# The v projection of layer 1 as seven products: differences of token rows in place, an earlier load of the second weights, and sums in pairs ahead of their splits

## The chip, the cores and the metric

One core of a Trainium2 chip runs the whole program. The metric is the device time of one execution in microseconds (us). The engines are named as in the profile: PE is TensorE (its matmuls), PEld its weight loads, DVE is VectorE, ACT is ScalarE, POOL is GpSimd, SP is SyncE, which only issues DMAs here. Each engine works through its own queue in order, and semaphores make one wait for another.

## The reference, cut to what matters

The program is a trunk of two layers over 1024 tokens of width 1024. The change touches the beginning of layer 1, where `v` is projected, and the end of layer 0 only in so far as it prepares that.

```
def rms_norm(x, g):
    y = xf * lax.rsqrt(jnp.mean(xf * xf, axis=-1, keepdims=True) + EPS)
    return (y * g.astype(jnp.float32)).astype(x.dtype)
...
            x = x + y @ w_out_a[j]          # end of layer 0
        else:
            h = rms_norm(x, norm_c[j])
            z = h @ w_in_c[j]               # 1024 x 6144
            u, v, g = split_cols(z, (GMLP_WIDTH, GMLP_WIDTH, GMLP_WIDTH))
            v = layer_norm(v, ln_v_g[j], ln_v_b[j])
```

## The kernel before, in words

All large products are kept in float32 accuracy by splitting each operand into a high part in fp32r and the rest (`hi` by an ACT cast, `lo` by a DVE subtraction), and by three matmuls for each product (`mm3`, lines 143 to 146).

**The output projection of layer 0** (`winograd`, lines 737 to 857) uses seven products of quarter matrices where eight would be plain, in 14 turns of 48 matmuls. In its last turns the residual rows `x1` become final. `x1_done` (line 991) stores a finished token tile of 128 rows to `x1dram`, has ACT square and sum it, and leaves the root (POOL) and the multiplication `norm_mul` (DVE, in place, line 187) to `norms_step`, which runs behind later groups of matmuls. Tiles 0 to 3 are finished first and are transposed for layer 1 by `norm_c_transpose` (into `gh` and `gl`). Tiles 4 to 7 are finished in the last turn, 13.

**The v projection** (`v_chunk`, lines 1122 to 1162) runs twice (`vc` 0 and 1), each time for 1024 of the 2048 columns and again with seven products in place of eight. A product has 48 matmuls of 128 x 512: four token tiles (`m`) by four slices of depth by three. I number them P0 to P6. P0 and P1 take the transposed tokens of tiles 0 to 3 (b11, b21); P2 to P6 take t1, t2, b22, t3 and t4, where t1 is the difference of tiles 4 to 7 and tiles 0 to 3 in the first half of the depth, b22 the second half of tiles 4 to 7, t2 = b22 - t1, t3 = t2 - b11 and t4 = b21 - t2. They are made while the products run:

- `token_tile(c)` (line 1085), behind each `m` of P0, takes a DVE difference `diff` of two rows, eight PE transposes into two PSUM banks (`ptd`), an ACT copy of t1 (`t1w`), t2 on DVE, and the splits of t1, b22 and t2.
- `token_less(i, c)` (line 1104) makes t3 (`i` = 2) or t4 (`i` = 3) for one tile with two DVE subtractions and a split.
- `make(i)` (line 1027) makes the weights of product `i` before product `i`-1 starts: for products 2 to 5 a DVE sum of quarters of `w_in_c`, then the split, for each of two halves `j` in turn.
- `fetch` (line 1016) loads the quarters of `w_in_c`: a12, a22, a21, and "sum", which holds the values of a21 at first and is overwritten with the running sums.

The order on ACT, DVE, POOL and SP is the order in which the code issues it (`manual_schedule`), and PE's is the program order. The two dictionaries `steps` (lines 1218 to 1238) say behind which product and token tile each helper is issued.

Of the kernel before, what the change touches and what calls it, by code (L numbers as in the profile page):

```python
# [62 lines left out]
def trunk_kernel(  # L63
# [945 lines left out]
    def v_weights(vc):  # L1009
# [6 lines left out]
        def fetch(*names):  # L1016
            for name in names:
                if name == "sum":
                    whole = big_tile(F32, f"vx{vc}").rearrange("p (j k s) -> p j k s", j=2, k=2)
                    q["sum"] = load_quarter(lambda j: whole[:, j], w_in_c, 0, nh + 1)  # L1020
                else:
                    d, kh = int(name[1]) - 1, int(name[2]) - 1
                    q[name] = load_quarter(
                        lambda j: late["vp"].tile([P, 2, 512], F32, tag="braw", name=f"v{vc}{name}_{j}", bufs=4),
                        w_in_c, kh * 512, nh + d)
# [96 lines left out]
    def v_chunk(vc, ops, steps):  # L1122
# [11 lines left out]
        for i, (bank_set, adds, bop, (d, th), act) in enumerate(products):  # L1134
# [4 lines left out]
            for m in range(4):  # L1139
# [18 lines left out]
                if i in (1, 6):  # L1158
# [1 line left out]
                if i in (5, 6):  # L1160
                    stats(*((0, 1) if i == 5 else (1, 1)), m)
                run(steps.get((i, m), []))
# [308 lines left out]
```

## Time and profile before

| | |
|---|---|
| median of 3 runs | 1345.37 us (1344.26 to 1346.29) |
| the profiled execution: its time | 1346.6 us |
| its span (first to last instruction) | 1344.9 us |
| PE busy | 1307.4 us, 97% of the span |
| PEld, DVE, ACT, POOL busy | 81%, 72%, 51%, 18% |
| mean granted clock of PE | 0.992 of full speed |

The profiled execution took 1.2 us more than the median of the runs, and 1.7 us lie around its span. PE is the engine that nearly fills the span. A stretch of the timeline matters for the time in so far as PE stands idle in it or is granted less than its full clock (1.0 is 2.4 GHz, 0.5 is 1.2 GHz).

### The profile page before, as it was taken

Reading aid. Unit: us, or ns where it says so; the run is one execution under the profiler, and the core shown is the slowest. Engines: PE = TensorE matmul, PEld = TensorE weight load, DVE = VectorE, ACT = ScalarE, POOL = GpSimd, SP = SyncE. Lnnn points to the kernel's source line nnn. Section 1 sums busy time; section 2 is a strip of 40 time slices with the busy share of each in tenths; the row PEclk is TensorE's granted clock in tenths of the full one; section 3 lists DMA queues with packets and bytes.
Section 4 is the critical chain, followed back from the end, with each engine's and each line's share of the span. In section 5 each row is a group of like instructions: output and inputs, shape, how many; then the busy total and the mean of one; then the engine's idle time right before and its main releaser. Section 6 shows DMA issues by size and latency. Waiting matters only on the chain.

```text
span 1344.9 us, 16867 instructions
## 1 busy us (share of the span) xinstructions
PE 1307.4 (97%) x6247; PEld 1091.4 (81%) x6247; DVE 974.2 (72%) x1571; ACT 691.7 (51%) x1245; POOL 236.5 (18%) x240
## 2 busy tenths in 40 slices
PE   7999999999999999999969999999999999999998
PEld 6988888888878888788757788788888888888887
DVE  6568787877678898978757856676666656579874
ACT  6467777786497786344443332444434444433431
POOL 3346565655223222000000000000000000000000
PEclk9999999999999999999979899999999999999999
DMA  6111010211311106313311523413333233596131
GB/s 224 32 48 53 27 54 26 57 39 33 97 33 51 36 17 254 125 61 127 126 63 63 171 80 118 149 67 113 103 110 106 75 110 102 183 372 243 48 110 63
DMA packets 99982, 133.41 MB, mean 99 GB/s; under 512 B 5163, under 2 KB 68796, under 8 KB 97852
## 3 DMA queue, kind: packets, MB, share of 16 engines
q1 hardware_dynamic: 99900, 132.34, 29.5%
q8 instruction: 49, 0.80, 0.3%
q14 instruction: 33, 0.27, 0.1%
HBM read 107.13 MB, written 25.19 MB: 98 GB/s over the span
## 4 chain that ended last, share of the span: by engine, by line
PE 70%; DVE 16%; ACT 8%; issue 3%; DMA 2%; SPq 0%; POOL 0%; DVEq 0%; ACTq 0%
PE m L144 6%; PE m L146 6%; PE m L145 6%; PE u L145 4%; PE u L146 4%; PE u L144 4%; PE g L144 4%; PE g L145 4%; PE g L146 4%; PE v L145 3%; PE v L144 3%; PE v L146 3%; PE s L1352 2%; DVE e L548 2%; PE gb L146 1%
## 5 line engine op out<-in xcount | busy, mean ns | idle before, releaser
L144 PE MATMUL m<-wh_w,wa 128*128 128x512 f32 x432 | 168.6, 390 | 1.4 <-DVE x L851 1.4
L146 PE MATMUL m<-wh_w,wa 128*128 128x512 f32 x432 | 168.1, 389 | 0.0
L145 PE MATMUL m<-wl_w,wa 128*128 128x512 f32 x432 | 168.1, 389 | 0.0
L144 PEld LDWEIGHTS m<-wh_w,wa 128*128 128x128 f32 x432 | 81.1, 188 | 19.0 <-ACT wa L716 1.8
L146 PEld LDWEIGHTS m<-wh_w,wa 128*128 128x128 f32 x432 | 81.1, 188 | 16.8
L145 PEld LDWEIGHTS m<-wl_w,wa 128*128 128x128 f32 x432 | 81.1, 188 | 16.6
L723 ACT CAST wh_w<-b 128x1024 fp32r<-128x1024 f32 x36 | 37.7, 1048 | 74.7 <-DVE b L818 54.2
L548 DVE CUSTOM_DVE_ANT_0 e<-ps,e,sink_bc 128x256 f32<-128x256 f32 (+1 forms) x128 | 61.9, 520 | 3.1 <-POOL e L523 2.6
L564 ACT ACTIVATE e<-e,nm 128x256 f32<-128x256 f32 (+1 forms) x128 | 61.4, 481 | 0.0
L851 DVE TENSOR_TENSOR x<-m,x 128x512 f32<-128x512 f32 x56 | 36.5, 684 | 29.2 <-PE m L146 29.2
L133 DVE TENSOR_TENSOR wl<-raw,wh 128x1024 fp32r<-128x1024 f32 x34 | 45.7, 1350 | 16.1 <-ACT wh L132 15.8
L1324 ACT ACTIVATE sg<-sg 128x512 f32<-128x512 f32 x24 | 15.2, 632 | 70.5 <-DVE sg L1323 70.5
L572 POOL TENSOR_TENSOR e<-e 128x512 f32<-128x512 f32 x28 | 37.2, 1327 | 80.3 <-ACT e L564 80.3
L144 PE MATMUL pq<-hh,wh 128*128 128x512 f32 x128 | 50.4, 394 | 0.0
L144 PE MATMUL ga<-hh,wh 128*128 128x512 f32 x128 | 50.1, 392 | 0.3 <-ACT z L871 0.3
L144 PE MATMUL gb<-hh,wh 128*128 128x512 f32 x128 | 50.1, 391 | 0.0
L724 DVE TENSOR_TENSOR wl_w<-b,wh_w 128x1024 fp32r<-128x1024 f32 x36 | 46.2, 1283 | 5.3 <-ACT wh_w L723 5.1
L146 PE MATMUL pq<-hh,wl 128*128 128x512 f32 x128 | 49.9, 390 | 0.0
L145 PE MATMUL pq<-hl,wh 128*128 128x512 f32 x128 | 49.9, 390 | 0.0
L146 PE MATMUL gb<-hh,wl 128*128 128x512 f32 x128 | 49.9, 390 | 0.0
L145 PE MATMUL gb<-hl,wh 128*128 128x512 f32 x128 | 49.9, 390 | 0.0
L146 PE MATMUL ga<-hh,wl 128*128 128x512 f32 x128 | 49.9, 389 | 0.0
(406 smaller groups left out, 3864.1 us busy)
## 6 DMA issues: line engine op xcount, KB each, us to landing
raw<-in_w_in_a_dram SPq DMA_DIRECT2D x34, 512.0 KB, 4.1
b<-in_w_out_a_dram SPq DMA_DIRECT2D x22, 512.0 KB, 3.5
b<-in_w_out_c_dram SPq DMA_DIRECT2D x22, 512.0 KB, 6.0
vdram<-v SPq DMA_DIRECT2D x32, 256.0 KB, 2.1
rawg<-in_w_in_c_dram SPq DMA_DIRECT2D x16, 512.0 KB, 4.7
rawu<-in_w_in_c_dram SPq DMA_DIRECT2D x16, 512.0 KB, 3.5
vg<-vdram SPq DMA_DIRECT2D x8, 1024.0 KB, 6.0
ydram<-ug SPq DMA_DIRECT2D x32, 256.0 KB, 2.4
```

Source lines behind the costliest of these rows:

```text
L133: nc.vector.tensor_tensor(out=lo, in0=raws[j], in1=hi.bitcast(F32), op=ALU.subtract)
L144: nc.tensor.matmul(acc, lhsT=lh, rhs=rh, start=first, stop=False, skip_group_check=shared)
L145: nc.tensor.matmul(acc, lhsT=lh, rhs=rl, start=False, stop=False, skip_group_check=shared)
L146: nc.tensor.matmul(acc, lhsT=ll, rhs=rh, start=False, stop=last, skip_group_check=shared)
L548: nc.vector.tensor_tensor_reduce(out=e[:, h, k0:256], in0=acc[:, j * 256:j * 256 + kw], in1=e[:, h, k0:256], scale=rs[:, 2 * (b % 4) + j:2 ...
L564: nc.scalar.activation(out=e[:, h], in_=e[:, h], func=AF.Exp, bias=st["nm"][:, h:h + 1], accum_out=st["sums"][:, h:h + 1])
L572: nc.gpsimd.tensor_tensor(out=p, in0=p, in1=e[:, :, P:256], op=ALU.add)
L723: nc.scalar.copy(out=hi, in_=src)
L724: nc.vector.tensor_tensor(out=lo, in0=src, in1=hi.bitcast(F32), op=ALU.subtract)
L851: nc.vector.tensor_tensor(out=dst, in0=accs[m], in1=dst, op=add)
L1324: nc.scalar.activation(out=c, in_=c, func=AF.Silu)
L1352: nc.tensor.matmul(acc[:, i * P:(i + 1) * P], lhsT=vgs[g][:, half * 4 + i, d * P:(d + 1) * P], rhs=ws_t[:, g, :], start=True, stop=True)
```

## The change

It does five things, for both chunks where both have them:

1. The difference of token rows is taken in place, on the first 512 columns of tiles 4 to 7, by the new `norm_c_finish`, directly behind their `norm_mul`. `token_tile` no longer has `diff`; its transposes read `x1` alone.
2. The quarter a12, the weights of P1, is loaded at turn 11 of the output projection, together with a11, into the large tile that "sum" had; "sum" goes to the smaller pool after the rows' stores. a21 is later loaded over a12, one product earlier than before.
3. `make(1)` is issued behind the second token tile instead of ahead of P0.
4. In `token_tile` the four splits stand in another order: b22's cast directly behind the copy of t1, t1's split later.
5. In `make` both halves are summed before both are split, and `token_less` takes several tiles, makes all their sums and then splits them, at fewer places. In P5 and P6 the layer norm's statistics (`stats`) change places, and stand behind the helpers.

```diff
+    def norm_c_finish(t, xt, r):
+
+        norm_mul(xt, xt, r, late["gain_c"])
+        if t >= 4:
+            nc.vector.tensor_tensor(out=xt[:, :512], in0=xt[:, :512], in1=x1_row(t - 4)[:, :512], op=ALU.subtract)
...
-                if name == "sum":
-                    whole = big_tile(F32, f"vx{vc}").rearrange("p (j k s) -> p j k s", j=2, k=2)
-                    q["sum"] = load_quarter(lambda j: whole[:, j], w_in_c, 0, nh + 1)
...
+                d, kh = (1, 0) if name == "sum" else (int(name[1]) - 1, int(name[2]) - 1)
+                if name == "a12":
+                    q["whole"] = big_tile(F32, f"vx{vc}").rearrange("p (j k s) -> p j k s", j=2, k=2)
+                if name in ("a12", "a21"):
+                    alloc = lambda j: q["whole"][:, j]
...
-            parts = []
-            for j in range(2):
-                if of:
-                    nc.vector.tensor_tensor(out=q[name][j], in0=q[of[0]][j], in1=q[of[1]][j], op=of[2])
-                parts.append(split_b(q[name][j], f"v{vc}_{i}_{j}"))
-            ops.append(parts)
+            for j in range(2 if of else 0):
+                nc.vector.tensor_tensor(out=q[name][j], in0=q[of[0]][j], in1=q[of[1]][j], op=of[2])
+            ops.append([split_b(q[name][j], f"v{vc}_{i}_{j}") for j in range(2)])
...
         if s == 11 and (j, m) == (0, 0):
             late["v"] = v_weights(0)
+            late["v"][2]("a12")
...
-        diff = token_rows(f"diff{c}").rearrange("p k s -> p (k s)")
-        nc.vector.tensor_tensor(out=diff, in0=row[:, :512], in1=other[:, :512], op=ALU.subtract)
...
         nc.scalar.copy(out=t1_rows, in_=t1)
+        b22h, b22l = [hs[1][1][:, :, c * P:(c + 1) * P] for hs in (h1h, h1l)]
+        nc.scalar.copy(out=b22h, in_=b22)
+        nc.vector.tensor_tensor(out=t2_whole[:, c], in0=b22, in1=t1_rows, op=ALU.subtract)
+        nc.vector.tensor_tensor(out=b22l, in0=b22, in1=b22h.bitcast(F32), op=ALU.subtract)
         token_split(0, c, t1)
-        nc.vector.tensor_tensor(out=t2_whole[:, c], in0=b22, in1=t1_rows, op=ALU.subtract)
-        token_parts((h1h[1][1], h1l[1][1]), c, b22)
         token_split(1, c, t2_whole[:, c])
...
-    def token_less(i, c):
+    def token_less(*which):
+
+        made = []
+        for i, c in which:
...
+            made.append((i, c, dst))
+        for args in made:
+            token_split(*args)
...
-    v_ops[2]("a12", "a22", "sum")
+    v_ops[2]("sum", "a22")
...
-        steps[4, -1].insert(0, (fetch, "a21"))
+        steps[3, -1].append((fetch, "a21"))
         if vc == 0:
+            del steps[0, -1]
             for c in range(4):
                 steps[0, c] = [(token_tile, c)]
-            for i, m, kind, c in ((2, 0, 2, 0), (2, 1, 2, 1), (2, 2, 2, 2), (3, 0, 2, 3), (3, 1, 3, 0), (3, 2, 3, 1),
-                                  (4, 1, 3, 2), (5, 0, 3, 3)):
-                steps[i, m] = [(token_less, kind, c)]
+            steps[0, 1].append((make, 1))
+            steps[2, 1] = [(token_less, (2, 0), (2, 1))]
+            steps[3, 1] = [(token_less, (2, 2), (2, 3), (3, 0))]
+            steps[4, 1] = [(token_less, (3, 1))]
+            steps[5, 1] = [(token_less, (3, 2))]
```

How the queues stand before and now, at the three places of which the prediction speaks. First DVE between the last rows of the output projection (`L851` adds a product to `x`) and the first token tile, where `L187` is the norm's multiplication and `L724` the lower half of a weight split. Before:

```order
L187 SCALAR_TENSOR_TENSOR x_5279<-x_5279,nrsc_6328,gain_c 128x1024
L161 TENSOR_SCALAR nmc_6351<-nssc_6341 128x1
L851 TENSOR_TENSOR x_5281<-m_3_5272,x_5281 128x512
L187 SCALAR_TENSOR_TENSOR x_5281<-x_5281,nrsc_6350,gain_c 128x1024
L161 TENSOR_SCALAR nmc_6367<-nssc_6363 128x1
L187 SCALAR_TENSOR_TENSOR x_5281<-x_5281,nrsc_6366,gain_c 128x1024
L724 TENSOR_TENSOR wl_v_1_0_6391<-v0a_0_6377,wh_v_1_0_6390 128x1024
L724 TENSOR_TENSOR wl_v_1_1_6395<-v0a_1_6379,wh_v_1_1_6394 128x1024
L1089 TENSOR_TENSOR diff_6413<-x_5279,x_5230 128x512
L1074 TENSOR_TENSOR t0l<-ptd_0_6415,t0h 128x4x128
```

The same place in the changed kernel, from the multiplication of tile 5 on (`L1004` is the new difference):

```order
L187 SCALAR_TENSOR_TENSOR x_5279<-x_5279,nrsc_6332,gain_c 128x1024
L1004 TENSOR_TENSOR x_5279<-x_5279,x_5230 128x512
L161 TENSOR_SCALAR nmc_6356<-nssc_6345 128x1
L851 TENSOR_TENSOR x_5281<-m_3_5272,x_5281 128x512
L187 SCALAR_TENSOR_TENSOR x_5281<-x_5281,nrsc_6355,gain_c 128x1024
L1004 TENSOR_TENSOR x_5281<-x_5281,x_5232 128x512
L161 TENSOR_SCALAR nmc_6373<-nssc_6368 128x1
L187 SCALAR_TENSOR_TENSOR x_5281<-x_5281,nrsc_6372,gain_c 128x1024
L1004 TENSOR_TENSOR x_5281<-x_5281,x_5232 128x512
L1103 TENSOR_TENSOR t2w<-ptd_1_6410,t1w_6421 128x512
```

The two weight splits and the separate difference are gone from the place ahead of the first token tile; a difference stands behind each multiplication, one of them ahead of the last `L851`.

Second, ACT in the token tiles 1 and 2 of the changed kernel (`L1161` copies a finished `m` of P0 out of PSUM, `L723` is the upper half of a weight split):

```order
L1100 COPY t1w_6459<-ptd_0_6449 128x512
L1102 CAST gh_6419<-ptd_1_6450 128x4x128
L1077 CAST t0h<-ptd_0_6449 128x4x128
L1077 CAST t1h<-t2w 128x4x128
L723 CAST wh_v_1_0_6468<-vx_6105 128x1024
L723 CAST wh_v_1_1_6472<-vx_6105 128x1024
L1161 COPY v_002_6489<-v_0_2_6476 128x512
L1100 COPY t1w_6501<-ptd_0_6491 128x512
L1102 CAST gh_6419<-ptd_1_6492 128x4x128
```

The casts of P1's weights, which stood ahead of all token tiles, stand between the second and the third, and `gh` has come ahead of `t0h`.

Third, DVE where the weights of P4 are made. Before:

```order
L1033 TENSOR_TENSOR vx_6385<-v0a_0_6377,vx_6385 128x1024
L724 TENSOR_TENSOR wl_v_4_0_6711<-vx_6385,wh_v_4_0_6710 128x1024
L1033 TENSOR_TENSOR vx_6385<-v0a_1_6379,vx_6385 128x1024
L724 TENSOR_TENSOR wl_v_4_1_6716<-vx_6385,wh_v_4_1_6715 128x1024
L1110 TENSOR_TENSOR t3w_6733<-t2w,gh_6203 128x512
```

Now:

```order
L1037 TENSOR_TENSOR v0sum_6384<-vx_6105,v0sum_6384 128x1024
L1037 TENSOR_TENSOR v0sum_6386<-vx_6105,v0sum_6386 128x1024
L724 TENSOR_TENSOR wl_v_4_0_6703<-v0sum_6384,wh_v_4_0_6702 128x1024
L724 TENSOR_TENSOR wl_v_4_1_6707<-v0sum_6386,wh_v_4_1_6706 128x1024
L1116 TENSOR_TENSOR t3w_6740<-t2w,gh_6206 128x512
```

The second sum has moved ahead of the first split, so that it stands where DVE waited for ACT's cast of the first half.

## Rows read from the trace of the kernel before

**Rows 1.** The page's 40 slices of 33.6 us each, two of its lines.
```profile
PE   7999999999999999999969999999999999999998
...
PEclk9999999999999999999979899999999999999999
```

**Rows 2.** Waits of PE, whole span: in all, times, longest (us).
```profile
PE ptd L1093 <- DVE diff L1089: 12.9, 3, 9.1
...
PE v L145 <- DVE wl_v L724: 2.5, 4, 0.8
PE v L144 <- ACT wh_v L723: 2.1, 3, 0.8
```

**Rows 3.** Windows: P0, P1, P2, P4, P5 of chunk 0, from first matmul to first matmul.
```profile
core 0: us, PE busy (x) PEld busy (x) DVE busy (x) ACT busy (x) POOL busy (x), PEclk, DMA share, GB/s
667.69:698.20 30.51, 17.54 (x81) 13.88 (x80) 17.17 (x24) 12.48 (x23) 1.10 (x2) 0.83 0.29 104
698.20:710.80 12.60, 12.60 (x52) 10.24 (x51) 8.66 (x11) 4.19 (x6) 0.00 (x0) 0.86 0.01 1
710.80:721.68 10.88, 10.88 (x50) 9.01 (x49) 8.46 (x11) 2.59 (x3) 0.00 (x0) 1.00 0.28 96
...
732.56:747.33 14.77, 11.90 (x50) 8.67 (x48) 10.27 (x14) 5.90 (x9) 0.00 (x0) 1.00 0.21 68
747.33:763.53 16.20, 14.48 (x49) 10.62 (x49) 13.60 (x18) 4.52 (x6) 0.00 (x0) 0.79 0.47 141
```

**Rows 4.** Timeline of PE: eight transposes between matmuls, and the first of `ptd`.
```profile
657.75 1.03 PE L202 MATMUL ptc<-ident,x 128*128 128x128 f32 x8
658.54 0.48 PE L144 MATMUL m<-wh_w,wa 128*128 128x512 f32 x1
...
679.68 1.09 PE L1093 MATMUL ptd<-ident,diff 128*128 128x128 f32 x4 [9.11 <-DVE diff L1089]
```

**Rows 5.** Timeline of DVE, 667 to 686 us: start, length, instruction [idle before].
```profile
667.95 1.28 DVE L187 SCALAR_TENSOR_TENSOR x<-x,nrsc,gain_c 128x1024 f32<-128x1024 f32 x1 [0.89 <-DMA x1dram<-x]
...
669.21 0.68 DVE L851 TENSOR_TENSOR x<-m,x 128x512 f32<-128x512 f32 x1
...
673.06 1.28 DVE L187 SCALAR_TENSOR_TENSOR x<-x,nrsc,gain_c 128x1024 f32<-128x1024 f32 x1 [1.68 <-DMA x1dram<-x]
676.32 1.23 DVE L724 TENSOR_TENSOR wl_v<-v0a,wh_v 128x1024 fp32r<-128x1024 f32 x1 [1.97 <-ACT wh_v L723]
...
678.85 0.68 DVE L1089 TENSOR_TENSOR diff<-x,x 128x512 f32<-128x512 f32 x1
...
684.45 0.68 DVE L1074 TENSOR_TENSOR t1l<-t2w,t1h 128x512 fp32r<-128x512 f32 x1
685.05 0.68 DVE L1089 TENSOR_TENSOR diff<-x,x 128x512 f32<-128x512 f32 x1
```

**Rows 6.** Timeline of ACT: weight casts, and the casts of token tile 0.
```profile
655.73 2.01 ACT L723 CAST wh_v<-va 128x1024 fp32r<-128x1024 f32 x2
...
675.24 1.04 ACT L723 CAST wh_v<-v0a 128x1024 fp32r<-128x1024 f32 x1 [4.10 <-DMA v0a<-in_w_in_c_dram]
...
680.80 0.59 ACT L1098 COPY t1w<-ptd 128x512 f32<-128x512 f32 x1 [2.64 <-PE ptd L1093]
681.28 0.59 ACT L1073 CAST t0h<-ptd 128x512 fp32r<-128x512 f32 x1
683.23 0.59 ACT L1073 CAST gh<-ptd 128x512 fp32r<-128x512 f32 x1 [1.35 <-DVE t2w L1100]
683.71 0.62 ACT L1073 CAST t1h<-t2w 128x512 fp32r<-128x512 f32 x1
```

**Rows 7.** Timeline of DVE, 730 to 760 us: splits alone and behind a sum.
```profile
732.14 1.23 DVE L724 TENSOR_TENSOR wl_v<-vx,wh_v 128x1024 fp32r<-128x1024 f32 x1 [1.18 <-ACT wh_v L723]
...
757.08 2.35 DVE L724 TENSOR_TENSOR wl_v<-v0a,wh_v 128x1024 fp32r<-128x1024 f32 x2
```

**Rows 8.** DMA issues, 640 to 800 us: count, KB each, median us to landing.
```profile
v0a<-in_w_in_c_dram SPq DMA_DIRECT2D x6, 512.0 KB, 4.3
...
v1a<-in_w_in_c_dram SPq DMA_DIRECT2D x4, 512.0 KB, 7.9
```

More of the change, by code (lines that the diff above doesn't have):

```diff
@@ L997, in x1_done @@
             norms.append([0, lambda: rs.append(norm_root(ss, f"c{t}")),
-                          lambda: norm_mul(xt, xt, rs[0], late["gain_c"])])
+                          lambda: norm_c_finish(t, xt, rs[0])])
+    def norm_c_finish(t, xt, r):
+        norm_mul(xt, xt, r, late["gain_c"])
+        if t >= 4:
+            nc.vector.tensor_tensor(out=xt[:, :512], in0=xt[:, :512], in1=x1_row(t - 4)[:, :512], op=ALU.subtract)
     norms = []
@@ L1017, in fetch @@
             for name in names:
-                if name == "sum":
-                    whole = big_tile(F32, f"vx{vc}").rearrange("p (j k s) -> p j k s", j=2, k=2)
-                    q["sum"] = load_quarter(lambda j: whole[:, j], w_in_c, 0, nh + 1)
-                else:
[L1022 to L1025, printed above, removed]
+                d, kh = (1, 0) if name == "sum" else (int(name[1]) - 1, int(name[2]) - 1)
[3 more added lines that the diff above has]
+                    alloc = lambda j: q["whole"][:, j]
+                else:
+                    alloc = lambda j: late["vp"].tile([P, 2, 512], F32, tag="braw", name=f"v{vc}{name}_{j}", bufs=4)
+                q[name] = load_quarter(alloc, w_in_c, kh * 512, nh + d)
         def make(i):
@@ L1085, in token_tile @@
     def token_tile(c):
-        row, other = x1_row(4 + c), x1_row(c)
-        diff = token_rows(f"diff{c}").rearrange("p k s -> p (k s)")
-        nc.vector.tensor_tensor(out=diff, in0=row[:, :512], in1=other[:, :512], op=ALU.subtract)
+        row = x1_row(4 + c)
         t1, b22 = [bank(f"ptd{c}_{i}").rearrange("p (k s) -> p k s", k=4) for i in range(2)]
-        for dst, src in ((t1, diff), (b22, row[:, 512:])):
-            for k in range(4):
-                nc.tensor.transpose(dst[:, k, :], src[:, k * P:(k + 1) * P], ident)
+        for i, dst in enumerate((t1, b22)):
+            for k in range(4 * i, 4 * i + 4):
+                nc.tensor.transpose(dst[:, k % 4, :], row[:, k * P:(k + 1) * P], ident)
         for hs, part in ((h1h, "h"), (h1l, "l")):
@@ L1157, in v_chunk @@
                         in_=dst.rearrange("p (g c) -> p g c", g=2))
[L1158 removed]
+                run(steps.get((i, m), []))
+                if i in (1, 5, 6):
                     stats(d, th, m)
[L1160 to L1162 removed]
+                if i == 6:
+                    stats(0, 1, m)
     def operand_b(name):
@@ L1218, in trunk_kernel @@
         steps = {(i, -1): [(make, i + 1)] for i in range(6)}
-        steps[4, -1].insert(0, (fetch, "a21"))
+        steps[3, -1].append((fetch, "a21"))
         if vc == 0:
+            del steps[0, -1]
             for c in range(4):
                 steps[0, c] = [(token_tile, c)]
-            for i, m, kind, c in ((2, 0, 2, 0), (2, 1, 2, 1), (2, 2, 2, 2), (3, 0, 2, 3), (3, 1, 3, 0), (3, 2, 3, 1),
-                                  (4, 1, 3, 2), (5, 0, 3, 3)):
-                steps[i, m] = [(token_less, kind, c)]
+            steps[0, 1].append((make, 1))
[3 more added lines that the diff above has]
+            steps[5, 1] = [(token_less, (3, 2))]
             def next_weights():
                 late["v"] = v_weights(1)
-                late["v"][2]("a12", "sum")
+                late["v"][2]("a12")
             steps[5, -1].append((next_weights,))
-            steps[6, -1] = [(lambda: late["v"][2]("a22"),), (lambda: late["v"][1](0),)]
+            steps[6, -1] = [(token_less, (3, 3)), (lambda: late["v"][2]("sum", "a22"),), (lambda: late["v"][1](0),)]
         else:
```

21 lines of the change are left out of this document (10 added, 11 removed).

## The prediction, made before the result was known

> **What bounds the kernel now.** I read the page's slices first. PE is busy in 97% of the span, so only PE's idle time and its slow stretches can be won, and the slices show one place for both: the 21st (from 672 us) has PE at 6 tenths, and the clock falls in the 21st and the 23rd [rows 1]. The waits of PE over the whole span name the cause: 12.9 us of transposes waiting for the DVE difference `diff`, the longest 9.1, and 4.6 us of matmuls of `v` waiting for the two halves of their weights [rows 2]. These are the longest waits of PE in the program, and all lie in chunk 0 of the v projection. So I cut that stretch into its seven products [rows 3]. P2, P3 and P6 take 10.88 us each at clock 1.00 (one of the three stands in the rows): 48 matmuls of 0.227 us, the floor. P0 takes 30.51, P1 12.60, P4 14.77 and P5 16.20. P0's floor is 10.88 and four times eight transposes; eight took 0.79 us (657.75 to 658.54) [rows 4], so 14.04. Over the floor are P0 by 16.47, P1 by 1.72, P4 by 3.89 and P5 by 5.32 us: 27.4 us, all that the change can win.
>
> **Why they are over it.** P0: the first `ptd` transpose starts at 679.68 after 9.11 us of idling [rows 4], since `diff` starts at 678.85, behind two weight splits of which the first starts at 676.32 [rows 5]. Those wait for ACT's cast at 675.24, and that for a load of a12 [rows 6]. But `diff` itself needs only a row that was long ready. P4 and P5: each half of the weights costs DVE a sum, then 1.18 us of waiting for ACT's cast, then the split [rows 7], and DVE, the engine behind, delivers late. P1: its clock is 0.86 at full PE busy [rows 3], so 1.72 us is a price of the low clock after PE stood.
>
> **The changed P0.** DVE's lengths are 0.68 us for 512 columns, 0.60 from start to start (684.45, 685.05), and 1.28 for a norm's multiplication [rows 5]; a split of 1024 takes 1.14 in a row of two (2.35 us together with 1.23 for the last [rows 7]). ACT: 0.59 for 512 columns, 0.48 from start to start (680.80, 681.28), 0.97 for a cast of 1024 in a row (2.01 for two) [rows 6].
> - The differences of tiles 4 and 5 stand behind their multiplications; the latter starts at 667.95 and gives its difference by 670.0 [rows 5]. So the transposes of token tiles 0 and 1 wait for nothing. The price: the last `L851`, now at 669.21, comes 0.7 us later, ends at 670.6, and everything behind it moves: the store of tile 7, and with it the last multiplication, which waited until 673.06 for that store, 3.17 us after `L851` ended. It now runs from 673.8 to 675.1.
> - ACT's first `t1w` can't start before that: its buffer takes the place of `gain_c`, which the last multiplication reads, and the built program waits for it. From 675.1 a chain of ACT and DVE runs, one round for a token tile: `t1w`, `gh` (ends 1.07 after the round began), `t2w` on DVE behind it (1.8), `t1h` and a copy (0.5 each): 2.8 us. Rounds 0 and 1 start at 675.1 and 677.9. Round 1's `t1h` is off ACT at 680.2; there the two casts for P1 now stand, 1.94, and then the copy, 0.5, so round 2 starts at 682.7; its `gh` ends at 683.8, its `t2w` at 684.4 and its `gl`, 0.6 behind, at 685.1.
> - PE meanwhile does P0 at its floor: 667.69 and 14.04 is 681.73. P1's first PSUM bank is the one that round 2's `gl` frees, so P1 starts at 685.15, after 3.4 us of idling, where it started at 698.20. **First term: 13.05 us.** Lower bound: the idling as it is with a round of each tile lengthened by 0.7 (2.1 us less); upper bound: P1 at 681.73 (3.4 more).
>
> What a PSUM bank allows sets the round. Today `gh` on ACT stood 1.35 us until `t2w` on DVE had ended, though both only read the bank [rows 6]; now `t2w` waits for `gh`. The Trainium skill, PSUM — Partial Sum Buffer, section PSUM bank collisions raise a hardware error, says that two engines must not read one bank together, and that programs are made to keep them apart. By that rule the new order gains nothing between the two reads; were they free to overlap, a round would be 0.5 shorter and the sum about 1.5 us larger. The trace agrees with the rule (the 1.35 us).
>
> **P1.** PE will have stood 3.4 us before it, more than ahead of today's P1, and less than the 9.11 before P0's slow matmuls. I keep P1 at 12.60: **second term 0**, between 1.72 (no fall) and -1.7 (a slow stretch twice as long).
>
> **P4 and P5.** P1 then ends at 697.75. DVE adds its last tile and takes its statistics (1.3), makes P3's weights in four operations of 1.14 (4.6), two tiles of t3 (four subtractions of 0.7 and two splits of 0.6: 4.0), and P4's weights (4.6): 712.3. P4 starts at 685.15 + 12.60 + 21.76 = 719.5. The weights are 7 us early where they were 4 us late. Three more differences with splits (6.0) and P5's weights (4.6) give 722.9 against 730.4 for P5. **Third term: 3.89 + 5.32 = 9.21**; lower bound 0, if the lateness stays. Pairing alone saves 1.18 us for each of the four pairs by then; the larger part is that PE no longer has DVE's delay of P0 behind it.
>
> **What is moved and costs nothing.** a12 goes ahead on SP's queue, into the place of a load of the same size at the same point, so the rows' stores start as they did; its cover is that its data is asked for at 680, not at 675. "sum" and a22 are issued behind the stores as a12 and a22 were, and are wanted 15 us later, behind token tile 3. a21 now overwrites a12 and is issued when P4's sums are done, about 710, and wanted by P5's sums at about 718: 8 us, for a landing of 4.3 to 7.9 [rows 8]. If it is later, DVE stands at its head, with the additions of P4 behind it; P5 has 7.5 us to spare. The transposes and matmuls are as many as before; the copy of x in place adds no instruction. In chunk 1 PE waits for nothing today [rows 2], and its moves are shorter on DVE: 0.
>
> **Sum.** 13.05 + 0 + 9.21 = 22.3 us. The profiled execution took 1346.6, so 1324.3; the median of the runs is 1.2 lower, so I give **1323.1**. Everything behind P6 moves with PE.
>
> **Rivals.**
> - *Less idling ahead of P1, or no slow clock* (0.16): 1318.0 to 1321. For it: nothing needs the ACT chain but four PSUM banks. Against: the chain is counted from rows.
> - *DVE stays late for P4 or P5*, by the additions of P1 piled up behind token tile 3, or by a21 (0.18): 1325.5, and 1332.3 with the whole 9.21.
> - *It does not do what it says*: the first transposes still wait for DVE, as a wait on DVE's counter stands at a later instruction than the difference (0.04): P0 stays, 1336. Against: the order of DVE's queue, above.
> - *Slower* (0.02): PE's clock stays low. After the idling it was 0.86 of full over P1 and 0.79 over P5 [rows 3]. At half clock each matmul costs 0.227 more. If 98 of the 336 matmuls of P0 to P6 go so beyond today's, 22.3 us are eaten, and with twice that the kernel takes 1367. It decides from two whole products on. Against: P2, P3 and P6 ran whole at 1.00.
> - No change, by some of these in part (0.02).
>
> The Trainium skill, TensorE: Matmul & The Clock Gate, section A second HAM failure mode: psum-queue depth-cycling, says that small idle times between groups of matmuls can make the clock swing between its two levels, and that the swings themselves cost. The trace agrees so far as the low stretches follow idle times; whether shorter idling makes more of them, no run here shows yet.
>
> **How the numbers follow.** The forecast, 1321 to 1325.5, has 0.58. The range adds most of the early case (from 1319) and half of the late one (to 1328.5), so 0.8. About 0.2% (2.7 us) is what a measurement can tell from no change. Faster by more: the first four cases, 0.96, of which I give one hundredth to what I haven't thought of. So 0.95, within 0.03, slower 0.02.
>
> **What would show it.** In the changed profile: no wait of PE for `L1004`; P0 in about 14 us; one wait of some 3.4 us ahead of P1, released by DVE's `gl`; P1 at a clock under 1; P2 to P6 at 10.88 each; P6's end some 22 us earlier. Wrong, if P4 or P5 show `wh_v` or `wl_v` waits again, if the wait ahead of P1 is over 6 us, or if chunk 1 gets waits that it has not today.

## The result, and the profile after

| | before | changed |
|---|---|---|
| median of 4 runs, us | 1345.83 (1344.26 to 1348.63) | 1326.38 (1326.35 to 1328.15) |
| profiled execution, span, us | 1346.6, 1344.9 | 1326.35, 1324.6 |
| PE busy, us (share) | 1307.4 (97%) | 1300.7 (98%) |
| mean granted clock of PE | 0.992 | 0.999 |

The changed kernel takes 0.9857 of the time of before (95% interval 0.9838 to 0.9875), 19.5 us less. The forecast was 1323.1, with a range of 1319.0 to 1328.5: the direction and the range held, and the gain was 3 us smaller than forecast. Two lines of the page's slices, to be held against [rows 1]:

```profile
PE   7999999999999999999999999999999999999998
...
PEclk9999999999999999999999999999999999999999
```

The 6 in the 21st slice is gone, and no slice has a clock under 9 tenths. The waits of PE over the whole span, in all, times, longest, stand against [rows 2]; the first is new, the second was 1.4 us in all before and the third 1.0:

```profile
PE v L144 <- ACT t1h L1077: 3.1, 1, 3.1
PE m L144 <- DVE x L851: 2.4, 2, 2.3
...
PE g L144 <- ACT sg L1329: 1.2, 1, 1.2
```

No transpose of `ptd` waits any more, and no product of `v` waits for its weights. The windows of the changed kernel for P0, P1, P2, P4 and P5 (time, PE, PEld, DVE, ACT and POOL busy, PE's clock, DMA) answer to [rows 3]:

```profile
670.74:688.46 17.72, 14.60 (x82) 12.27 (x80) 15.17 (x22) 11.85 (x22) 1.10 (x2) 1.00 0.50 178
688.46:699.46 11.00, 11.00 (x49) 9.08 (x50) 10.58 (x14) 4.57 (x7) 0.00 (x0) 1.00 0.08 25
699.46:710.34 10.88, 10.88 (x50) 9.01 (x49) 10.65 (x15) 4.42 (x7) 0.00 (x0) 1.00 0.21 74
...
721.22:732.10 10.88, 10.88 (x50) 9.01 (x49) 8.72 (x11) 5.32 (x6) 0.00 (x0) 1.00 0.18 60
732.10:742.98 10.88, 10.88 (x50) 9.01 (x49) 8.75 (x12) 0.62 (x1) 0.00 (x0) 1.00 0.85 278
```

| us | P0 | P1 | P4 | P5 | P0 to P6's end |
|---|---|---|---|---|---|
| before | 30.51 | 12.60 | 14.77 | 16.20 | 106.72 |
| forecast | 17.46 | 12.60 | 10.88 | 10.88 | 84.46 |
| changed | 17.72 | 11.00 | 10.88 | 10.88 | 83.12 |

So the seven products won 23.60 us, 1.3 more than the 22.3 forecast. But P0 starts at 670.74, where it started at 667.69: 3.05 us were lost ahead of everything that the change edits. Another 0.3 went behind P6, in two waits (the third line above is 0.1 to 0.2 longer, and 0.2 of the second line is new). 23.60 - 3.05 - 0.3 is the difference of the spans, 20.2 to 20.3. Most of the 3.05 lies in one place of the output projection, shown by the timeline of PE (start, length, instruction, idle before):

```profile
556.61 0.47 PE L144 MATMUL m<-wh_w,wa 128*128 128x512 f32 x1 [2.26 <-DVE x L851]
556.91 0.41 PE L145 MATMUL m<-wl_w,wa 128*128 128x512 f32 x1
557.14 0.60 PE L146 MATMUL m<-wh_w,wa 128*128 128x512 f32 x1
557.55 0.63 PE L144 MATMUL m<-wh_w,wa 128*128 128x512 f32 x1
557.98 0.63 PE L145 MATMUL m<-wl_w,wa 128*128 128x512 f32 x1
```

PE waits 2.26 us (1.43 before), and the matmuls behind it start 0.43 us apart where 0.23 is usual: PE's clock is at its lower level, 1.2 GHz, until 560.5. Together 0.9 of later start and 1.5 of slow matmuls; the other 0.6 were there from the program's first 25 us. Is this the change's doing, or chance? And did the gain come from where the prediction saw it? The runs below were made for these two questions.

### The profile page after: what moved, and what is told of

Same layout as the page of the kernel before. It is cut to its first block, busy times and chain, and to the rows that moved or that the text cites. A ratio compares the mean times of both kernels' runs of the same rounds, so it can differ in the third digit from the quotient of the medians.

```text
span 1324.6 us, 16851 instructions
## 1 busy us (share of the span) xinstructions
PE 1300.7 (98%) x6247; PEld 1089.3 (82%) x6247; DVE 974.4 (74%) x1571; ACT 691.0 (52%) x1245; POOL 236.2 (18%) x240
## 4 chain that ended last, share of the span: by engine, by line
PE 75%; DVE 12%; ACT 7%; DMA 3%; issue 3%; SPq 0%; DVEq 0%; ACTq 0%
PE m L144 6%; PE m L146 6%; PE m L145 6%; PE u L146 4%; PE u L145 4%; PE u L144 4%; PE v L144 4%; PE v L145 4%; PE v L146 4%; PE g L144 4%; PE g L145 4%; PE g L146 4%; PE s L1363 2%; PE pk L269 2%; PE pq L144 2%
## 5 line engine op out<-in xcount | busy, mean ns | idle before, releaser
L723 ACT CAST wh_w<-b 128x1024 fp32r<-128x1024 f32 x36 | 37.7, 1047 | 74.0 <-DVE b L818 52.5
L851 DVE TENSOR_TENSOR x<-m,x 128x512 f32<-128x512 f32 x56 | 36.5, 685 | 29.2 <-PE m L146 29.2
L724 DVE TENSOR_TENSOR wl_w<-b,wh_w 128x1024 fp32r<-128x1024 f32 x36 | 46.2, 1284 | 6.1 <-ACT wh_w L723 5.9
```

The costliest lines, as they stand in the source:

```text
L723: nc.scalar.copy(out=hi, in_=src)
L724: nc.vector.tensor_tensor(out=lo, in0=src, in1=hi.bitcast(F32), op=ALU.subtract)
L851: nc.vector.tensor_tensor(out=dst, in0=accs[m], in1=dst, op=add)
```

## The experiments

Each kernel was timed beside the kernel before on the same chip, four to six times. All ratios are to that kernel; P0 to P5 are from the profiled execution.

| run | median (lowest to highest), us | ratio, 95% interval | P0 starts | P0 | P1 | P4 | P5 |
|---|---|---|---|---|---|---|---|
| e1, the change again | 1325.64 (1323.31 to 1325.86) | 0.9841 (0.9827 to 0.9855) | 667.86 | 18.12 | 12.34 | 10.88 | 10.88 |
| e2, difference late | 1332.18 (1331.01 to 1332.32) | 0.9892 (0.9879 to 0.9905) | 667.55 | 25.55 | 11.01 | 10.88 | 10.88 |
| e3, part 5 undone | 1333.04 (1331.76 to 1334.68) | 0.9901 (0.9887 to 0.9915) | 667.94 | 18.02 | 12.63 | 14.31 | 14.18 |
| e4, part 5 alone | 1336.85 (1335.92 to 1339.16) | 0.9932 (0.9919 to 0.9944) | 667.62 | 30.79 | 11.03 | 10.88 | 10.88 |
| e5, part 3 undone | 1323.96 (1323.24 to 1324.90) | 0.9835 (0.9821 to 0.9850) | 667.70 | 17.03 | 10.99 | 10.88 | 10.88 |
| e6, parts 2 and 3 undone | 1325.49 (1325.11 to 1326.30) | 0.9847 (0.9833 to 0.9862) | 667.51 | 19.78 | 11.00 | 10.88 | 10.88 |
| e7, part 4 undone | 1326.27 (1326.03 to 1328.06) | 0.9857 (0.9840 to 0.9873) | 667.66 | 19.20 | 12.66 | 10.88 | 10.88 |
| e8, of part 5 only `make` | 1326.02 (1324.47 to 1326.51) | 0.9848 (0.9834 to 0.9863) | 668.07 | 18.15 | 12.57 | 10.88 | 10.88 |
| e9, P1's splits in tile 2 | 1324.57 (1321.91 to 1324.82) | 0.9831 (0.9816 to 0.9845) | 667.93 | 16.29 | 13.45 | 10.88 | 10.88 |
| e10, e9 and the last row later | 1322.08 (1321.77 to 1322.37) | 0.9818 (0.9804 to 0.9831) | 667.78 | 14.78 | 11.80 | 10.88 | 10.88 |
| e11, the change again | 1324.43 (1323.68 to 1327.70) | 0.9840 (0.9824 to 0.9856) | 667.65 | 17.66 | 10.98 | 10.88 | 10.88 |
| e12, long pause | 1334.37 (1333.74 to 1335.20) | 0.9909 (0.9896 to 0.9923) | 670.35 | 25.13 | 13.11 | 10.88 | 10.88 |

e1 to e4 ran on one chip, e5 to e8 on one, e9 to e12 on one. In all of them P2, P3 and P6 take 10.88.

### e1 and e11: the changed kernel again

No edit. What was expected of e1:

> The changed kernel once more, unedited. Its profile had P0's first matmul at 670.74 us, 3.05 us later than before, with a 2.26 us wait of PE near 556 us and a stretch of slow matmuls behind it, all far ahead of the first edited instruction. Theory chance (the loads of that stage land a little later in one execution than in another): another profile shows P0's first matmul anywhere from 667.5 to 671, and a median that may move by up to 3 us. Theory program (the changed kernel always has it): 670.7 again, 1326.4. Both: P1 11.0 us, P2 to P6 10.88 each, one wait of about 3.1 us ahead of P1.

And of e11:

> The changed kernel unedited, for comparison on the same chip: 1325.6 where PE's clock falls once behind a pause, 1323.3 where it does not, P1 accordingly 12.4 or 11.0 us.

Windows of P0 and P1, of e1:

```profile
667.86:685.98 18.12, 14.95 (x82) 12.28 (x80) 15.30 (x22) 11.84 (x22) 1.10 (x2) 0.98 0.49 174
685.98:698.32 12.34, 12.34 (x49) 10.08 (x49) 11.89 (x16) 4.57 (x7) 0.00 (x0) 0.88 0.13 43
```

and of e11:

```profile
667.65:685.31 17.66, 14.60 (x81) 12.26 (x80) 15.16 (x22) 11.84 (x22) 1.10 (x2) 1.00 0.50 179
685.31:696.29 10.98, 10.98 (x48) 9.09 (x49) 10.56 (x14) 4.58 (x7) 0.00 (x0) 1.00 0.08 25
```

P0 starts at 667.9 and 667.7, where the same program had 670.74. The wait near 556 us was 1.72 and 1.43, with no slow matmul behind it. The 3.05 us were chance, as the first theory of e1 had it. What differs in that execution is a load of the output projection's weights: ACT's cast of them starts at 537.50, where it started at 536.02 in the profile before, and DVE and PE are late behind it.

P1 is the second thing that differs with the program unchanged: 11.00 in the first profile, 12.34 in e1 (11.0 was expected by both sides), 10.98 in e11. So an execution costs about 1323.5 where the clock never falls (1323.31, 1323.68 and 1323.73 among the twelve, the three with a mean clock of 1.000), some 2 us more where the mean is 0.999 (one fall in the profiles that show it), and some 4 us more in the two with 0.997. The twelve executions have a median of 1325.75.

### e2: the difference back in `token_tile`

```diff
-                          lambda: norm_c_finish(t, xt, rs[0])])
+                          lambda: norm_mul(xt, xt, rs[0], late["gain_c"])])
...
-        row = x1_row(4 + c)
+        row, other = x1_row(4 + c), x1_row(c)
+        nc.vector.tensor_tensor(out=row[:, :512], in0=row[:, :512], in1=other[:, :512], op=ALU.subtract)
```

> Part 1 undone: the difference is taken in token_tile, still in place. Theory (the place of the difference bounds P0): the first transposes wait for the last norm_mul and their difference, some 4 us after the first four token tiles' matmuls, and each later token tile waits for the splits of the one before; P1 starts about 5 us later, and the time is 1331.5 (1330 to 1335, more if PE's clock falls again). Rival (moving make(1) out of the way was what mattered): the transposes wait under 1 us, 1326 to 1327.5.

1332.18, 6.5 over e1 on the same chip; the theory holds. PE's waits in the stretch of P0, in all, times, longest:

```profile
PE ptd L1096 <- DVE x L1092: 8.1, 3, 5.2
```

Behind the 5.2 us PE's clock falls as well: P0 has PE busy for 17.44 us in place of 14.60. Both come from a difference of 0.68 us of DVE that stands in the wrong place of the queue. Of the 12.8 us by which P0 became shorter, undoing part 1 alone gives back 7.4 to 7.9 (25.55 against 18.12 in e1 and 17.66 in e11): with parts 2 to 4 in place the first transposes wait 5.2 us, not 9.1.

### e3, e4 and e8: sums in pairs

e3 undoes part 5, e4 makes part 5 alone on the kernel before (its edit is e3's, read the other way). The edit of e3:

```diff
-            for j in range(2 if of else 0):
-                nc.vector.tensor_tensor(out=q[name][j], in0=q[of[0]][j], in1=q[of[1]][j], op=of[2])
-            ops.append([split_b(q[name][j], f"v{vc}_{i}_{j}") for j in range(2)])
+            parts = []
+            for j in range(2):
+                if of:
+                    nc.vector.tensor_tensor(out=q[name][j], in0=q[of[0]][j], in1=q[of[1]][j], op=of[2])
+                parts.append(split_b(q[name][j], f"v{vc}_{i}_{j}"))
+            ops.append(parts)
...
-            steps[2, 1] = [(token_less, (2, 0), (2, 1))]
-            steps[3, 1] = [(token_less, (2, 2), (2, 3), (3, 0))]
-            steps[4, 1] = [(token_less, (3, 1))]
-            steps[5, 1] = [(token_less, (3, 2))]
+            for i, m, kind, c in ((2, 0, 2, 0), (2, 1, 2, 1), (2, 2, 2, 2), (3, 0, 2, 3), (3, 1, 3, 0), (3, 2, 3, 1),
+                                  (4, 1, 3, 2), (5, 0, 3, 3)):
+                steps[i, m] = [(token_less, (kind, c))]
```

e8 makes only the second half of this edit, with the statistics back in their old places as well (as in e3), and leaves `make` with its pairs.

> Part 5 undone, in make, token_less, its places and the statistics. Theory of the prediction (P4 and P5 were late mostly because the head's delay on DVE was carried on): 1326.4 to 1330. Rival, from the two traces (DVE starts the weights of P2 4.2 us behind P1's start before and 3.8 us now, so the head carries nothing on, and the order of sums and splits is all of it): P4 and P5 are late again by 9 us or a little more, as P1 no longer has a slow stretch, 1335 to 1338.

> Part 5 alone, on the kernel before. Theory of the prediction (the head's delay makes P4 and P5 late): they stay late by 4 us or more together, 1340 to 1345. Rival (the order of sums and splits is all of it): P4 and P5 take 10.88 us each, 1336 to 1337, and P0 stays at 30.5 us.

> Of part 5 only make's pairs stay; token_less one tile at a time at the old places, the statistics as before. Theory (by the changed kernel's trace P4's weights are ready 5.6 us and P5's 6.0 us early, and the old helpers cost DVE 4.1 us by P4 and 6.2 us by P5): P4 on time, P5 up to 1 us late, 1325.6 to 1327. Rival (the helpers' places are worth as much as the pairs): P4 or P5 late by 3 us or more, 1328.5 to 1332.

In e3 the lateness is back. Its windows of P4 and P5:

```profile
720.35:734.66 14.31, 11.89 (x50) 8.67 (x48) 9.81 (x14) 5.89 (x9) 0.00 (x0) 1.00 0.20 64
734.66:748.84 14.18, 11.85 (x48) 9.03 (x49) 12.26 (x16) 3.56 (x4) 0.00 (x0) 1.00 0.42 120
```

3.43 and 3.30 us over the floor, 6.7 together, and 7.4 us in the medians (1333.04 against 1325.64). That lies between the two sides of its expectation: the lateness is as the rival has it, but smaller than its 9 us. In e4 it is gone although P0 is as bad as ever. Its windows of P0, P4 and P5:

```profile
667.62:698.41 30.79, 19.25 (x81) 15.44 (x80) 17.17 (x24) 12.48 (x23) 1.10 (x2) 0.78 0.29 103
...
731.20:742.08 10.88, 10.88 (x50) 9.01 (x49) 8.96 (x11) 5.31 (x6) 0.00 (x0) 1.00 0.17 57
742.08:752.96 10.88, 10.88 (x50) 9.01 (x49) 8.74 (x12) 0.62 (x1) 0.00 (x0) 1.00 0.91 302
```

1336.85 is 9.7 below the kernel before, as e4's rival had it. So the delay of P0 (the head) does not make P4 and P5 late. Nor does it add to their waits: PE's idle time in the two is 4.59 us in the kernel before (14.77 - 11.90 and 16.20 - 14.48 [rows 3]) and 4.75 in e3, whose P0 is short. The 2.5 us by which 9.21 exceeds 6.7 come from matmuls at the low clock in P5 (PE busy for 14.48 us at clock 0.79 before, 11.85 at 1.00 in e3). The reason can be read on DVE, where the weights of P4 are made. e3:

```profile
717.13 1.22 DVE L1039 TENSOR_TENSOR v0sum<-vx,v0sum 128x1024 f32<-128x1024 f32 x1
719.47 1.23 DVE L724 TENSOR_TENSOR wl_v<-v0sum,wh_v 128x1024 fp32r<-128x1024 f32 x1 [1.11 <-ACT wh_v L723]
720.61 1.22 DVE L1039 TENSOR_TENSOR v0sum<-vx,v0sum 128x1024 f32<-128x1024 f32 x1
722.99 1.23 DVE L724 TENSOR_TENSOR wl_v<-v0sum,wh_v 128x1024 fp32r<-128x1024 f32 x1 [1.17 <-ACT wh_v L723]
```

and the changed kernel:

```profile
710.88 2.35 DVE L1037 TENSOR_TENSOR v0sum<-vx,v0sum 128x1024 f32<-128x1024 f32 x2
713.28 2.36 DVE L724 TENSOR_TENSOR wl_v<-v0sum,wh_v 128x1024 fp32r<-128x1024 f32 x2
```

Two waits of 1.1 to 1.2 us, one for each half, are gone: ACT casts the first half while DVE sums the second. From the first sum of P2's weights to the last split of P4's DVE takes 34.5 us in e3 (689.77 to 724.22) and 23.4 in the changed kernel (692.26 to 715.64): six such waits (6.8), and the helpers' own waits and one helper that now stands behind.

e8 tells how much of that was needed. Its last splits for P4 and P5:

```profile
715.47 2.42 DVE L724 TENSOR_TENSOR wl_v<-v0sum,wh_v 128x1024 fp32r<-128x1024 f32 x2
...
728.32 2.36 DVE L724 TENSOR_TENSOR wl_v<-vx,wh_v 128x1024 fp32r<-128x1024 f32 x2
```

They end at 717.9 and 730.7, and P4 and P5 start at 720.55 and 731.43: early by 2.7 and by 0.8 us. 1326.02 is the changed kernel's time. The pairs of weights pay for all; the helpers' pairs and places only add reserve that nothing uses, 2.9 us for P4 and 5.3 for P5 (in the changed kernel the weights are ready 5.6 and 6.0 us early). e8's theory held, P5 a little better than it had it.

### e5 and e6: when P1's weights are loaded and made

e5 issues `make(1)` ahead of P0 again; e6 also loads a12 behind the rows' stores again.

```diff
-            del steps[0, -1]
...
-            steps[0, 1].append((make, 1))
```

and for e6 moreover (with a21 and "sum" in their old tiles and places)

```diff
-            late["v"][2]("a12")
...
-    v_ops[2]("sum", "a22")
+    v_ops[2]("a12", "a22", "sum")
```

> Part 3 undone: make(1) ahead of P0 again, with a12 still loaded early. Theory (the chain to P1 is as long either way): ACT casts P1's weights while it waits for gain_c's release, DVE's two splits push token tile 0 back by 1.9 us, and the third tile's chain is shorter by the two casts; P1 starts within 0.5 us of where it did, the wait ahead of it stays near 3.1 us, 1325.6 (1323 to 1326.5). Rival (the move is what lets the token tiles run): the wait grows by the 1.9 to 2.4 us of the splits, 1327.5 to 1328.

> Parts 2 and 3 undone: a12 loaded behind the rows' stores, make(1) ahead of P0, while the difference stays at the norm. Theory (the difference was what held the transposes, the load only the casts): no transposes wait; the casts end 2 us after gain_c is free, token tile 0 is 2.5 us later, the third tile's chain 1.9 us shorter; 1326 to 1327. Rival (the late load was the root of P0's idling): 1331 or more.

e5 came out faster than either side of its expectation in P0: P1 starts 17.03 us behind P0's start, not 17.66 to 18.12 as in e11 and e1. Its casts of P1's weights on ACT

```profile
657.64 1.06 ACT L723 CAST wh_v<-vx 128x1024 fp32r<-128x1024 f32 x1
...
666.59 1.05 ACT L723 CAST wh_v<-vx 128x1024 fp32r<-128x1024 f32 x1 [1.00 <-ACT gh L207]
```

and the two waits of PE that are left in P0 and at P1's start

```profile
679.06 0.63 PE L1095 MATMUL ptd<-ident,x 128*128 128x128 f32 x4 [0.80 <-DVE gl L1104]
...
684.73 0.47 PE L144 MATMUL v<-wh_v,gh 128*128 128x512 f32 x1 [1.28 <-DVE gl L1104]
```

show why: with a12 loaded early, the built order has the casts and splits inside the last turn of the output projection, among gaps of ACT and DVE, and not at P0's head, as I had taken for granted. They are off the chain to P1, and 3.1 us of waiting become 2.1. Part 3 of the change gives away 0.6 to 1.1 us in P0. The median, 1323.96, lies in the range of e5's theory, whose reason did not hold.

In e6 no transposes wait for a difference, and the rival's 1331 did not come. The casts wait for the load, and the chain moves the wait from P1 to the second half of the third token tile's transposes:

```profile
676.22 1.05 ACT L723 CAST wh_v<-v0a 128x1024 fp32r<-128x1024 f32 x1 [4.19 <-DMA v0a<-in_w_in_c_dram]
```

```profile
681.61 0.75 PE L1094 MATMUL ptd<-ident,x 128*128 128x128 f32 x4 [3.56 <-DVE gl L1103]
```

P0 and P1 take 30.78 us together, with a fall of the clock within P0; e1 has 30.46 with a fall within P1. So parts 2 and 3 together are worth a few tenths of a us, and in the medians (1325.49 against 1325.64 and 1324.43) nothing that can be told. The median is half a microsecond under the range of e6's theory.

### e7: the order of the splits in a token tile

```diff
-        b22h, b22l = [hs[1][1][:, :, c * P:(c + 1) * P] for hs in (h1h, h1l)]
-        nc.scalar.copy(out=b22h, in_=b22)
-        nc.vector.tensor_tensor(out=t2_whole[:, c], in0=b22, in1=t1_rows, op=ALU.subtract)
-        nc.vector.tensor_tensor(out=b22l, in0=b22, in1=b22h.bitcast(F32), op=ALU.subtract)
         token_split(0, c, t1)
+        nc.vector.tensor_tensor(out=t2_whole[:, c], in0=b22, in1=t1_rows, op=ALU.subtract)
+        token_parts((h1h[1][1], h1l[1][1]), c, b22)
```

> Part 4 undone: the four splits of token_tile in the old order. Theory (the chain of ACT and DVE sets P1's start, and the old order makes a round 0.5 us longer and has the third tile's gl at its end): P1 starts 2.4 us later, the wait ahead of it is about 5.5 us, 1328 (1327 to 1330). Rival (the order within a tile is hidden): 1325.6.

P1 starts 1.1 us later than in e1 (19.20 against 18.12), not 2.4, and 1326.27 lies between the two sides of the expectation. A round from `t1w` to `t1w` is 3.9 us, 1.1 longer than now, as ACT's `gh` stands behind `t2w` again. What I had wrong is which bank P1 waits for. ACT, DVE and PE of e7:

```profile
677.70 0.59 ACT L1077 CAST gh<-ptd 128x512 fp32r<-128x512 f32 x1 [1.35 <-DVE t2w L1102]
...
688.05 0.69 DVE L1078 TENSOR_TENSOR gl<-ptd,gh 128x512 fp32r<-128x512 f32 x1 [0.65 <-ACT gh L1077]
```

```profile
686.86 0.50 PE L144 MATMUL v<-wh_v,gh 128*128 128x512 f32 x1 [3.15 <-DVE t0l L1078]
```

PE starts 1.2 us before the third tile's `gl` does, directly behind that tile's `t0l` (686.11 to 686.80): in the old order the bank of t1 is done first, and by these rows P1 takes that one. Part 4 is worth about 1 us, within the spread of the medians (1326.27 against 1325.64 and 1324.43).

### e9 and e10: the rest of the wait

e9 runs `make(1)` in token tile 2, between the split of b22 and those of t1 and t2. e10 also moves the last row's multiplication and difference behind token tile 0, done in two halves, with the gain loaded a second time into two small tiles, since the first copy's pool is closed by then.

```diff
-    def token_tile(c):
+    def token_tile(c, *between):
...
+        run(between)
         token_split(0, c, t1)
...
-                steps[0, c] = [(token_tile, c)]
+                steps[0, c] = [(token_tile, c, *([(make, 1)] if c == 2 else []))]
-            steps[0, 1].append((make, 1))
```

and for e10 moreover

```diff
-             out_a_after, lambda: [norms_step(0) for _ in range(2)])
+             out_a_after, lambda: norms_step(0))
...
+    late["gain_7"] = [vp.tile([P, 512], F32, tag="vst", name=f"gain7_{i}", bufs=12) for i in range(2)]
+    for i in range(2):
+        nc.sync.dma_start(out=late["gain_7"][i], in_=rows_bc(norm_c[0, i * 512:(i + 1) * 512], 512))
...
+            steps[0, 0].append((norms_step, 0))
```

> The changed kernel with P1's casts and splits moved into token tile 2, between the split of b22 and those of t1 and t2. Theory (two casts and two splits stand in the chain to P1's first bank, 1.9 us): P1's first wait is about 1.2 us in place of 3.1, with another 0.7 us at most for wl_v; PE's clock keeps its level or not as it comes; 1323 to 1325. Rival (the splits then come too late): the wait is only moved from gl to wl_v, 1325.6.

> As e9, and the last row's multiplication and difference moved behind token tile 0, with a second copy of the gain loaded for it, so that no token tile's buffer waits for that multiplication. Theory (the chain starts 3.4 us earlier and P1's inputs are all ready): no wait of PE between P0's first matmul and P6's end over 0.5 us, P0 14.4 us, 1321 (1320 to 1323). Rival (DVE, which has 10 us of work for three tiles, the row and the splits, becomes the bound): P1 waits 1 to 2 us for wl_v or gl, 1322 to 1324.

PE's two waits of e9:

```profile
684.22 0.47 PE L144 MATMUL v<-wh_v,gh 128*128 128x512 f32 x1 [1.26 <-DVE gl L1104]
685.26 0.50 PE L145 MATMUL v<-wl_v,gh 128*128 128x512 f32 x1 [0.57 <-DVE wl_v L724]
```

are the 1.2 and 0.7 of its theory, but the clock fell all the same, and P1 took 13.45:

```profile
684.22:697.67 13.45, 12.88 (x49) 10.22 (x49) 13.38 (x17) 6.09 (x10) 0.00 (x0) 0.87 0.08 28
```

In e10 the windows of P0 and P1

```profile
667.78:682.56 14.78, 14.60 (x82) 12.27 (x80) 13.02 (x21) 10.11 (x19) 1.10 (x2) 1.00 0.73 249
682.56:694.36 11.80, 11.23 (x49) 9.09 (x49) 11.77 (x15) 6.10 (x10) 0.00 (x0) 1.00 0.00 1
```

show the first wait nearly gone (0.18 us), the second as it was (0.57, for `wl_v`) and the clock at 1.00. Its first `t1w` on ACT

```profile
672.44 0.59 ACT L1104 COPY t1w<-ptd 128x512 f32<-128x512 f32 x1
```

starts 4.66 us behind P0's start, where it started 7.61 behind in the changed kernel (678.35 - 670.74). 1322.08 is 2.35 us under e11 on the same chip, and each of its four executions is under each of e11's. It beats both kernels. It lies in the ranges of both sides of e10's expectation: the theory's wait of at most 0.5 us was missed by little, and the rival's wait for `wl_v` is there, but shorter than its 1 to 2 us. What is left is 0.9 us over the floor in P1.

### e12: a longer pause

```diff
-        nc.scalar.copy(out=t1_rows, in_=t1)
+        for _ in range(13 if c == 2 else 1):
+            nc.scalar.copy(out=t1_rows, in_=t1)
```

> The changed kernel with twelve more copies of t1w in token tile 2 on ACT (the same data again), so that the wait ahead of P1 is about 8.9 us in place of 3.1. Theory (a longer pause makes the slow stretch behind it longer): P1 takes 13.5 to 14.5 us, 1332 to 1334. Rival (a slow stretch behind a pause has one length): P1 takes 12.3 to 12.7 us, 1331 to 1331.6, and 11.0 us if the clock does not fall at all, 1329.5.

The copies took 0.61 us each, not 0.48, and PE waited 10.53 us. P1's window

```profile
695.48:708.59 13.11, 13.11 (x49) 10.63 (x49) 12.02 (x16) 4.58 (x7) 0.00 (x0) 0.83 0.13 44
```

has 2.1 us over the 11.0 of an undisturbed P1; behind pauses of 3.2 us it was 1.3 to 1.7. So P1 lies between the two sides: by this one profile the cost grows with the pause, but far less than in proportion. One reason stands in the pause itself, whose last 5.6 us have this window:

```profile
689.80:695.40 5.60, 0.00 (x0) 0.00 (x0) 1.36 (x3) 5.14 (x11) 0.00 (x0) 0.50 0.00 0
```

The clock is at its lower level already while PE stands, and that part of the slow stretch costs nothing. This execution also had the late load and the slow matmuls near 556 us (P0 starts at 670.35). Its 1335.2 us stand against 1323.68 of e11's profiled execution: 7.5 more in P0, 2.1 in P1, 2.7 of P0's later start, and 0.8 less behind P6.

## Why the prediction was right, and where it was not

- **P0: right, with its mechanism.** P1 started 17.72 us behind P0, 17.46 was forecast. The chain stands in the rows as it was counted, here DVE of the changed kernel

```profile
676.98 1.28 DVE L187 SCALAR_TENSOR_TENSOR x<-x,nrsc,gain_c 128x1024 f32<-128x1024 f32 x1 [1.50 <-DMA x1dram<-x]
678.30 0.69 DVE L1004 TENSOR_TENSOR x<-x,x 128x512 f32<-128x512 f32 x1
679.45 0.69 DVE L1103 TENSOR_TENSOR t2w<-ptd,t1w 128x512 f32<-128x512 f32 x1 [0.46 <-ACT gh L1102]
...
687.63 0.68 DVE L1104 TENSOR_TENSOR gl<-ptd,gh 128x512 fp32r<-128x512 f32 x1
```

  and ACT:

```profile
678.35 0.59 ACT L1100 COPY t1w<-ptd 128x512 f32<-128x512 f32 x1 [3.35 <-PE ptd L1095]
...
683.54 1.99 ACT L723 CAST wh_v<-vx 128x1024 fp32r<-128x1024 f32 x2
...
685.92 0.58 ACT L1100 COPY t1w<-ptd 128x512 f32<-128x512 f32 x1
```

  `t1w` starts when the last multiplication has read the gain (676.98 + 1.28 = 678.26), the rounds are 2.83 us, the two casts stand before the third, and PE starts 0.2 us behind the third `gl`. The view of waits names `t1h` for this, and `PE ptd` for `t1w`; both names are inferred, and the rows speak against both. `t1h` is no input of P1, and e5's same wait is put down to `gl`. The transposes of token tile 0 start at 673.46 and take 1.03 us, and e5's same wait of `t1w` is put down to the multiplication:

```profile
676.51 0.59 ACT L1100 COPY t1w<-ptd 128x512 f32<-128x512 f32 x1 [3.31 <-DVE x L187]
```

  e10 shows it by an experiment: with that multiplication out of the way `t1w` starts 3 us earlier. The difference in place was worth 6.5 us (e2), and the order in a tile about 1 (e7). The parts do not add up: without part 1, parts 2 to 4 still bring P0 from 30.51 to 25.55, and with it, undoing parts 2 and 3 costs a few tenths (e6). With part 5 alone (e4) the time is 11.2 us above e1. Two readings of the prediction were off and moved nothing: PE is busy for at least 14.60 us in P0 (the changed kernel, e10 and e11), not for 14.04, but the chain and not the floor sets P1's start; and the waits for `diff` and for the weights are not all of "the longest waits of PE in the program", as PE stands for 8.5 us at the start of the program, ahead of its first transposes (line 202).
- **The order of reads in a bank.** What the prediction drew from the Trainium skill, PSUM — Partial Sum Buffer, section PSUM bank collisions raise a hardware error, agrees with the runs: in the old order ACT's read waited for DVE's (1.35 us in e7), in the new one DVE's `t2w` follows ACT's `gh`, and never do the two overlap. Both built programs have a wait there, so no run tells what the bank itself would do.
- **P1: the term 0 was mis-sized, by chance of the execution.** "I keep P1 at 12.60" was right for e1 (12.34), e3, e7 and e8, and wrong for the first profile and e11 (11.0): luck either way. Of the six profiles with a wait of 3.06 to 3.17 us ahead of P1, four have a fall of the clock behind it and two have none. The first profile had its fall near 556 us instead. In spans the forecast was 1344.9 - 22.3 = 1322.6, and 1324.6 came: 3.05 more ahead of P0, 1.3 less in the products, 0.3 more behind them. The other 1.2 us between 1323.1 and 1326.38 is the excess of the profiled execution over its median, which I took off and which the changed kernel's does not have.
- **P4 and P5: the right number for the wrong reason.** The step that failed is "Pairing alone saves 1.18 us for each of the four pairs by then; the larger part is that PE no longer has DVE's delay of P0 behind it". A pair saves two such waits, one for each half; and DVE began P2's weights 4.16 us behind P1's start before and 3.80 behind it now, which the trace of before could have told. The first sum of P2's weights, before and in the changed kernel:

```profile
702.36 1.22 DVE L1033 TENSOR_TENSOR vx<-vx,v0a 128x1024 f32<-128x1024 f32 x1
...
692.26 2.35 DVE L1037 TENSOR_TENSOR v0sum<-v0sum,v0a 128x1024 f32<-128x1024 f32 x2
```

  DVE had nearly the same lag to PE, and all of the lateness grew after it. e4 shows it by itself: 9.7 us with P0 left as it was. The term also priced the low clock in P5 as DVE's lateness; that it went with the waits made the number right.
- **What costs nothing: right.** a21's load over a12 and the moved loads made no wait (10.88 for P4 to P6 in the three profiles of the changed kernel). What I gave no thought to is a small loss behind P6, 0.3 to 0.8 us in the three profiles of the changed kernel, in two waits (of `g` for ACT's `sg`, of `m` for DVE's `x`) that are together longer in the two where PE comes earlier; what holds them was not tried.
- **The rivals.** "No slow clock" came in some executions, but at 1323.5 and not at 1318 to 1321, for the 1.2 us above and the loss behind P6. That DVE stays late for P4 or P5, or that the transposes still wait, did not come. The slower case, a clock that stays low, was not seen in any run: a fall cost 1.3 to 3 us. The Trainium skill, TensorE: Matmul & The Clock Gate, section A second HAM failure mode: psum-queue depth-cycling, says that small idle times can set the clock swinging. In the changed kernel and its edits the clock fell at most once in P0 and P1 and was back before P1's end. The kernel before and e4 have two falls there (behind waits of 9.11 and 1.93, and of 9.22 and 1.89 us). No run shows more of a cycle than that.

## What to carry to other kernels

Where one engine sums and another casts what it has summed, sum all halves first and split them afterwards: two waits in each helper, none of them on PE, were worth 9.7 us (e4) in products whose weights DVE makes later; e8 shows that the pairs of weights alone do it. Before you put a late stage down to an earlier one, compare the lag of the engine that delivers behind the one that waits at both places: lags that are nearly equal acquit the earlier stage. And a wait that is named by its last-ended producer should be held against what the instruction needs: here the name was an operand of a later product.

## What the runs showed of the hardware that was not expected

Whether the granted clock falls is not decided by the length of the pause ahead of it alone: behind 3.06 and 3.12 us it stayed at 1.00, behind 3.15, 3.16 and twice 3.17 it fell, and in e9 it fell at a P1 that had paused for 1.26 and 0.57 us; near 556 us it fell in both executions that waited 2.26 or more, and in none that waited 1.72 or less. Behind the wait ahead of the third token tile's transposes it stayed in the kernel before (1.90 us) and fell in e4 (1.89 us). Between waits for weights of up to 0.84 us each, it fell in P5 of the kernel before and stayed in P4 and P5 of e3. A fall shows as some six to ten matmuls at 0.43 us. It cost 1.3 to 1.7 us behind the pauses of 1.3 to 3.6 us, 2.1 in e12, 2.6 in P5 of the kernel before (PE busy for 14.48 us, 11.85 in e3), and 2.8 to 2.9 behind the pauses of 5.2 and 9.1 us in P0 of e2 and of the kernel before (17.44 and 17.54 us, not 14.60). This alone makes two executions of one program differ by 2 us, as much as the smaller parts of this change are worth; why it falls in one and not in the next stays open.
